# A transformer-like layer on one core: waits of the branch pool by tile, and block weights split ahead of output weights

## The chip, the cores and the metric

The kernel runs on one core of one Trainium2 chip. The metric is the device time of one execution in microseconds; the table below has it for three runs. Five engines share the work: TensorE (PE) multiplies, VectorE (DVE) and ScalarE (ACT) do elementwise work, GpSimd (POOL) a little of it, and SyncE (SP) issues nearly all DMAs. Each engine works through its own instructions in the order in which the program gives them, and waits on semaphores for the others.

## The reference

One layer with 512 tokens (T), width 1024 (D) and a hidden width of 2816 (FF), in fp32:

```
mod = silu(c) @ w_ada + b_ada                 # nine vectors: shifts, scales, gates
u = rms_norm(x) * (1 + sc1) + sh1
x = x + 0.5 * g1 * swiglu(u, ffn1_w_in, ffn1_w_out)
u = rms_norm(x) * (1 + sc2) + sh2
z = u @ w_mix + b_mix                         # q, k, v of two attentions, and gates
y_a = sigmoid(o) * rms_norm(mlstm(...))       # chunkwise mLSTM, 4 heads
y_b = forgetting_attention(...)               # 16 heads
merged = sigmoid(g_a) * (y_a @ w_branch_a) + sigmoid(g_b) * (y_b @ w_branch_b)
x = x + g2 * (merged @ w_out)
u = rms_norm(x) * (1 + sc3) + sh3
x = x + 0.5 * g3 * swiglu(u, ffn2_w_in, ffn2_w_out)
# swiglu(u, w_in, w_out) = (silu(u @ w_in_a) * (u @ w_in_b)) @ w_out
```

## The kernel before

**Products in three parts.** Each fp32 operand is split into a rounded part (hi) and a remainder (lo); a product is three matmuls, hi x hi, hi x lo and lo x hi (`mm3`, L112 to L114). For a weight, `w_stat` loads a tile `raw` of 128x1024 (three buffers, L82) and `split` (L85) makes `wh` on ScalarE (L93) and `wl` on VectorE (L95), four buffers each.

**Feed-forward stages.** FF is cut into 22 blocks of 128. `block` (L553) takes the two input weights of a block (one for each half of `w_in`), multiplies the tokens by both, 24 matmuls each, and `hidden` makes silu(a) * b of it, `hp` (L376, L377). Two blocks form a pair, whose product with the output weights saves multiplications by sums of its quarters (as in Strassen's scheme). For pair jj, `weight_load` (L404) loads the pair's output weights, 1 MB, into `rw`, which has one buffer. `weight_sums` (L414 to L422) rounds the first half of them (`wh`, `wl`) and forms four differences in place. `sums_store` (L427) writes three quarters of the tile to the DRAM buffer `S_d`, for use later. The next pair's load into `rw` can start when that store has been done. `pair_sums` (L382 to L398) makes sums and splits of `hp`. `first_products` (L434 on) multiplies them with `wh` and with the first difference. In between, `steps` puts accumulations of modulation weights (`raw` from `w_ada`, `acc`, L303 to L305) on VectorE.

`three_blocks` handles pairs 0 to 2 of the first feed-forward stage: blocks 0 to 2 are computed with the input stage, then come blocks 3, 4 and 5. `ffn_pairs` handles the others, and all of the second stage.

**Mixing and branches.** After attention, `ya` and `yb` hold the two branch inputs, eight tiles of 128x512 each. `gate(m, i)` computes a tile of the gates and stores it in DRAM (`g_d`); gate (7, 1) is the last. `split_y` (L1160, L1161) splits a branch's input. `branch(m, i)` loads a gate tile (`sg`) and multiplies the split input by a branch weight, 24 matmuls; there are eight for each branch, the first branch with y_a. These tiles live in the pool `br`, which takes the memory of the attention pools before it.

**What sets the order.** A scheduler orders the instructions of each engine from the program's order and its own rules; `issue_after(x)` puts the instructions in its scope behind x. A pool that takes over memory makes its tiles wait for the work that used it: by default for the earlier pool's work as a whole, with `reuse_waits="tile"` for that of the tiles that lay there.

Of the kernel before, what the change touches and what calls it, by code (L numbers as in the profile page):

```python
# [11 lines left out]
F32 = mybir.dt.float32  # L12
F32R = mybir.dt.float32r
# [7 lines left out]
P = 128  # L21
# [27 lines left out]
class Layer:  # L49
# [35 lines left out]
    def split(self, src, shape, eng=None, hi_v=False):  # L85
        nc = self.nc
        hi = self.wp.tile(shape, F32R, name=self.nm("wh"), tag="wh", bufs=4)
        lo = self.wp.tile(shape, F32R, name=self.nm("wl"), tag="wl", bufs=4)
        if hi_v:
            nc.vector.tensor_copy(hi, src)  # L90
        else:
            with self.tc.issue_after(self.last_uf.ins) if self.lo_after else nullcontext():
                nc.scalar.activation(hi, src, AF.Copy)  # L93
        with self.tc.issue_after(self.lo_after) if self.lo_after else nullcontext():
            self.last_lo = (eng or nc.vector).tensor_tensor(lo, src, hi, op=SUB)  # L95
        return hi, lo
# [453 lines left out]
    def block_w(self, w_in, j):  # L550
        return self.w_stat(w_in, j * P), self.w_stat(w_in, FF + j * P)

# [43 lines left out]
    def ffn_pairs(self, w_in, w_out, j0, steps, n):  # L596

        for jj in range(j0, NP):
            if jj:
                self.block(w_in, 2 * jj)  # L600
# [12 lines left out]
        self.first_products(NP - 1)  # L613
# [167 lines left out]
    def gates(self, mp, yp):  # L781
# [31 lines left out]
        def columns():  # L813
            b = self.tbank()
            for tb in range(NT):
                nc.tensor.transpose(b[:, tb * 64:(tb + 1) * 64], gm[:, tb * P:(tb + 1) * P], self.ident[:64, :64])
            self.gcol = yp.tile([P, NT, 64], F32, name="gcol")
            nc.vector.tensor_copy(self.gcol, b[:, 0:256].rearrange("p (b c) -> p b c", b=NT))
        return columns
# [44 lines left out]
    def v_mlstm(self, half, ap, ip):  # L864
# [3 lines left out]
        for i in range(2):  # L868
            pair = [ap.tile([P, NT, 258], F32R, name=self.nm("vm"), tag="vm", bufs=6) for _ in range(2)]
# [19 lines left out]
    def mlstm_w(self, h, ip):  # L889
# [7 lines left out]
        nc.gpsimd.tensor_tensor(b4(Mm), b4(Mb), self.maskM[:, None, :].to_broadcast([P, NT, P]), op=ADD)  # L897
        W = ip.tile([P, 1280], F32, name=self.nm("W"), tag="p6", bufs=5)
        Wh = ip.tile([P, 1280], F32R, name=self.nm("Wh"), tag="p6", bufs=5)
        Wl = ip.tile([P, 1280], F32R, name=self.nm("Wl"), tag="p6", bufs=5)  # L900
        for sb in range(NT):
# [46 lines left out]
    def fox_qkv(self, g, ip):  # L948
# [28 lines left out]
        bv = self.bias_bcast([(VF + o, 256)], ip)  # L977
        vt = [ip.tile([P, NT, 2, P], F32R, name=self.nm("fvt"), tag="vm", bufs=6) for _ in range(2)]
        def donev(tb, ps):
# [47 lines left out]
    def fox_s(self, h, ip):  # L1027
# [7 lines left out]
        nc.gpsimd.tensor_tensor(b4(Am), b4(A0), self.maskF[:, None, :].to_broadcast([P, NT, P]), op=ADD)  # L1035
        S = ip.tile([P, 1280], F32, name=self.nm("S"), tag="p6", bufs=5)
        mn = sp.tile([P, NT, 2], F32, name=self.nm("mn"), tag="mn", bufs=4)
# [19 lines left out]
    def fox_p(self, h, ip):  # L1057
# [7 lines left out]
        Ph = ip.tile([P, 1408], F32R, name=self.nm("Ph"), tag="p6", bufs=5)  # L1065
        Pl = ip.tile([P, 1408], F32R, name=self.nm("Pl"), tag="p6", bufs=5)
        nc.scalar.activation(Ph[:, 512:640], self.ident, AF.Copy, scale=0.0)
# [62 lines left out]
    def gate(self, m, i, ip):  # L1130
        nc = self.nc
        ps = self.gbank()
        w = self.w_stat(self.A["w_mix"][0], (GA, GB)[i] + m * P)
        self.gemm_stat(ps, w, 0, T, range(0, 4))
        yield
        self.gemm_stat(ps, w, 0, T, range(4, 8))
        th = self.tmp(ip, "tg")
        nc.scalar.activation(th, ps, AF.Tanh, scale=0.5, bias=self.hgg[:, 8 * i + m:8 * i + m + 1])
        nc.sync.dma_start(self.g_d[8 * i + m], th)
        yield  # L1140


    def branch(self, m, i, bp, dst):
# [4 lines left out]
        wh, wl = self.w_stat(A[("w_branch_a", "w_branch_b")[i]][0], m * P)  # L1148
        for k in range(NK):
            self.mm3(ps, wh[:, k, :], wl[:, k, :], self.y[k][0], self.y[k][1], k == 0, k == NK - 1)  # L1150
        dst = sg if dst is None else dst
        nc.vector.scalar_tensor_tensor(dst, sg, 1.0, ps, op0=ADD, op1=MUL)
        return dst

    def split_y(self, ys, tile):
        nc = self.nc
        out = []
        for i, y in enumerate(ys):
            hi, lo = tile(i, 0), tile(i, 1)
# [6 lines left out]
    def run(self):  # L1166
# [8 lines left out]
        with tc.tile_pool(name="f1t", bufs=1) as tp:  # L1175
# [39 lines left out]
        with tc.tile_pool(name="gates", bufs=1) as mp:  # L1215
# [5 lines left out]
            for m in range(4, 8):  # L1221
# [5 lines left out]
                self.qk_conv(m, ps, yp, mp)  # L1227
        with tc.tile_pool(name="att", bufs=1) as ip:
            self.maskM = ip.tile([P, P], F32, name="maskM")
# [8 lines left out]
            nc.gpsimd.memset(self.onz[:, :, 1:2], 0.0)  # L1238
            self.hom = ip.tile([P, NK], F32, name="hom")
            nc.vector.tensor_scalar(self.hom, self.colA[:, R_OM:R_OM + NK], 0.5, None, op0=MUL)  # L1240
            self.hgg = ip.tile([P, 2 * NK], F32, name="hgg")
            nc.vector.tensor_scalar(self.hgg, self.colA[:, R_GG:R_GG + 2 * NK], 0.5, None, op0=MUL)
# [44 lines left out]
        self.ntmp, self.xn_tiles = 4, self.xn_branch  # L1287
        with tc.tile_pool(name="br", bufs=1) as bp:
            self.tp = bp
            self.mh = [bp.tile([P, T], F32R, name=f"mh{m}") for m in range(NK)]  # L1290
            self.ml = [bp.tile([P, T], F32R, name=f"ml{m}") for m in range(NK)]
            halves = lambda: [yp.tile([P, 512], F32, name=self.nm("acc"), tag="qk", bufs=16) for _ in range(2)]
            steps = self.ada_steps((6, 7), halves, self.tbank)
            ya = self.split_y(self.ya, lambda i, lo: bp.tile([P, T], F32R, name=self.nm("yl"), tag=f"y{lo}", bufs=8))
            ta = []
# [66 lines left out]
```

## Time and profile before

| | |
|---|---|
| device time, median of 3 runs | 1353.15 us (1352.94 to 1353.87) |
| the profiled execution: device time, span | 1355.86 us, 1354.1 us |
| TensorE busy, its mean granted clock | 1321.2 us (98%), 0.989 |
| VectorE, ScalarE, GpSimd busy | 936.4 us (69%), 619.4 us (46%), 135.2 us (10%) |
| DMA, mean | 171 GB/s |

The span runs from the first to the last instruction of the profiled execution. Busy shares are means over stages that have different limits, so the rows further down are taken from single stages. The granted clock is TensorE's clock as a share of full speed. In the stretch from 73 to 320 us the kernel is in the first feed-forward stage; the branches begin at 855 us, the second feed-forward stage at about 1010 us.

### The profile page before, as it was taken

The page shows a single profiled execution, that of the slowest core. Times are in us where ns is not written, and L with a number is a line of the kernel's source. Part 1 is how long each engine was busy: PE and PEld are TensorE (multiplying, and loading weights), DVE is VectorE, ACT ScalarE, POOL GpSimd, SP SyncE. Part 2 cuts the span into 40 slices and gives each one's busy share as a digit, 9 for nine tenths or more (in the row PEclk, how much of TensorE's full clock was granted, in tenths as well). Part 3 has the DMA queues.
Part 4 walks back from the last instruction along what each step waited for, and adds up shares of the span by engine and source line. Part 5 has one row for each costly group of instructions (what it writes and reads, how often), then busy time and mean ns, then how long its engine had stood idle before and what let it go on. Part 6 is the DMA issues. An engine that isn't in the chain of part 4 may idle for free.

```text
span 1354.1 us, 17890 instructions
## 1 busy us (share of the span) xinstructions
PE 1321.2 (98%) x6438; PEld 1107.6 (82%) x6438; DVE 936.4 (69%) x1697; ACT 619.4 (46%) x1050; POOL 135.2 (10%) x175
## 2 busy tenths in 40 slices
PE   6899999999999999999999999899999999999998
PEld 5787888888888888888888878688888888888887
DVE  6685778579677876876585886567677575555655
ACT  4442343336447655556565675323444343333442
POOL 2000000001011100313031311002110000000000
PEclk9899999999999999999999999899999999999999
DMA  9566877666762434444343442587526745435474
GB/s 314 153 204 209 255 234 239 220 199 231 243 171 78 135 112 123 124 117 127 81 140 86 114 131 73 189 251 229 171 94 219 240 151 186 145 124 176 131 263 146
DMA packets 224524, 231.10 MB, mean 171 GB/s; under 512 B 12274, under 2 KB 179858, under 8 KB 224436
## 3 DMA queue, kind: packets, MB, share of 16 engines
q1 hardware_dynamic: 221940, 224.61, 52.8%
q0 software_dynamic: 2432, 5.33, 1.1%
q8 instruction: 51, 0.84, 0.2%
q14 instruction: 37, 0.30, 0.1%
q10 hardware_dynamic: 64, 0.02, 0.0%
HBM read 199.97 MB, written 29.95 MB: 170 GB/s over the span
## 4 chain that ended last, share of the span: by engine, by line
PE 82%; DVE 8%; DMA 5%; ACT 3%; issue 2%; SPq 0%; POOL 0%; ACTq 0%; DVEq 0%; POOLq 0%
PE g L113 19%; PE g L114 19%; PE g L112 19%; PE t L461 2%; PE t L463 2%; PE t L462 2%; DMA rw<-in_ffn_w_out_dram 2%; PE g L760 2%; PE t L1102 2%; DVE wl L95 1%; PE t L436 1%; PE t L434 1%; PE t L435 1%; DMA raw<-in_ffn_w_in_dram 1%; PE t L1072 1%
## 5 line engine op out<-in xcount | busy, mean ns | idle before, releaser
L93 ACT ACTIVATE wh<-raw 128x1024 fp32r<-128x1024 f32 (+2 forms) x225 | 232.0, 1037 | 347.5 <-PE g L113 102.6
L95 DVE TENSOR_TENSOR wl<-raw,wh 128x1024 fp32r<-128x1024 f32 (+2 forms) x225 | 272.7, 1216 | 155.3 <-ACT wh L93 149.6
L114 PE MATMUL g<-uh,wl 128*128 128x512 f32 (+2 forms) x984 | 369.7, 377 | 2.3 <-DVE wl L95 2.3
L112 PE MATMUL g<-uh,wh 128*128 128x512 f32 (+2 forms) x984 | 370.2, 377 | 1.2 <-ACT wh L93 1.2
L113 PE MATMUL g<-ul,wh 128*128 128x512 f32 (+2 forms) x984 | 370.0, 376 | 0.7 <-DVE ul L262 0.7
L114 PEld LDWEIGHTS g<-uh,wl 128*128 128x128 f32 (+1 forms) x984 | 184.8, 188 | 37.3 <-DVE wl L95 3.8
L112 PEld LDWEIGHTS g<-uh,wh 128*128 128x128 f32 (+1 forms) x984 | 184.7, 188 | 35.3 <-ACT wh L93 2.3
L113 PEld LDWEIGHTS g<-ul,wh 128*128 128x128 f32 (+1 forms) x984 | 185.0, 188 | 34.3 <-DVE ul L262 0.9
L112 PE MATMUL g<-wh,uh 128*128 128x512 f32 (+1 forms) x320 | 111.9, 350 | 0.0
L114 PE MATMUL g<-wh,ul 128*128 128x512 f32 (+1 forms) x320 | 111.1, 347 | 0.0
L113 PE MATMUL g<-wl,uh 128*128 128x512 f32 (+1 forms) x320 | 111.0, 347 | 0.0
L303 DVE SCALAR_TENSOR_TENSOR acc<-raw,ccol,acc 128x1024 f32<-128x1024 f32 (+1 forms) x63 | 65.9, 1062 | 28.7 <-DMA raw<-in_w_ada_dram 28.1
L377 DVE TENSOR_TENSOR hp<-g,sl 128x512 f32<-128x512 f32 x43 | 29.6, 689 | 56.6 <-PE g L114 55.5
L112 PEld LDWEIGHTS g<-wh,uh 128*128 128x128 f32 x320 | 60.5, 189 | 7.8 <-DVE tk L956 0.5
L114 PEld LDWEIGHTS g<-wh,ul 128*128 128x128 f32 x320 | 60.5, 189 | 7.7
L113 PEld LDWEIGHTS g<-wl,uh 128*128 128x128 f32 x320 | 60.6, 189 | 7.4
L112 PE MATMUL g<-yl,wh 128*128 128x512 f32 x128 | 51.2, 400 | 5.9 <-ACT yl L1160 5.9
L414 ACT ACTIVATE wh<-rw 128x1024 fp32r<-128x1024 f32 x22 | 23.3, 1059 | 63.5 <-PE g L113 36.0
L113 PE MATMUL g<-yl,wh 128*128 128x512 f32 x128 | 51.1, 399 | 0.0
L114 PE MATMUL g<-yl,wl 128*128 128x512 f32 x128 | 50.8, 397 | 0.0
L322 POOL DMA_DIRECT2D mod_d<-br x14 | 7.0, 501 | 387.3 <-DVE br L321 281.9
L1054 ACT ACTIVATE S<-S,mn 128x128 f32<-128x128 f32 (+1 forms) x64 | 35.5, 556 | 20.3 <-DVE mn L1046 12.6
(314 smaller groups left out, 2285.0 us busy)
## 6 DMA issues: line engine op xcount, KB each, us to landing
raw<-in_ffn_w_in_dram SPq DMA_DIRECT2D x82, 512.0 KB
raw<-in_w_ada_dram SPq DMA_DIRECT2D x56, 512.0 KB
raw<-in_w_mix_dram SPq DMA_DIRECT2D x48, 512.0 KB
rw<-in_ffn_w_out_dram SPq DMA_DIRECT2D x22, 1024.0 KB
S_d<-rw SPq DMA_DIRECT2D x22, 768.0 KB
raw<-S_d SPq DMA_DIRECT2D x30, 512.0 KB
raw<-in_w_mix_dram SPq DMA_DIRECT2D x32, 256.0 KB
ar<-in_w_ada_dram SPq DMA_DIRECT2D x14, 512.0 KB
```

What stands on the lines that cost most here:

```text
L93: nc.scalar.activation(hi, src, AF.Copy)
L95: self.last_lo = (eng or nc.vector).tensor_tensor(lo, src, hi, op=SUB)
L112: mm(ps, lh, rh, start=start, stop=False)
L113: mm(ps, lh, rl, start=False, stop=False)
L114: self.last_mm = mm(ps, ll, rh, start=False, stop=stop)
L303: nc.vector.scalar_tensor_tensor(a, r[:, cut(i)], self.ccol[:, k:k + 1], a, op0=MUL, op1=ADD)
L377: nc.vector.tensor_tensor(h, ps_b[:, c0:c1], s[:, :c1 - c0], op=MUL)
L461: mm(ps[t], a[0], wh[:, k, :], start=first and c + k == 0, stop=False, skip_group_check=True)
L462: mm(ps[t], a[0], wl[:, k, :], start=False, stop=False, skip_group_check=True)
L463: mm(ps[t], a[1], wh[:, k, :], start=False, stop=end, skip_group_check=True)
L760: mm = nc.tensor.matmul(acc_ps[b], (wl if p == 1 else wh)[:, b % 2, s], ul if p == 2 else uh, start=k == 0 and p == 0, stop=k == NK - 1 an ...
L1054: nc.scalar.activation(S[:, ws], S[:, ws], AF.Exp, scale=-1.0, bias=m, accum_out=sm[:, qb:qb + 1])
```

## The change

Three edits. In `three_blocks` and `ffn_pairs`, the input weights of the following block are loaded and split ahead of `weight_sums`, whose instructions are put behind the first rounding of that block's weights (`first_hi`); this holds for jj = 1 and 2 in the first stage and for jj = 0 in the second. The pool `br` waits tile by tile; gate (7, 1) is computed inside it, after the splits of y_a; the first branch weight is split ahead, and the tiles `mh`, `ml` are allocated later. The splits of y_b come in four parts of two, in the branch steps m = 1 to 4, behind the last tanh of the gates on ScalarE and behind the last y_a remainder on VectorE. Besides, some tiles move to other pools (`vp`, `yp`), and `gcol` shrinks from 64 to 36 columns.

```diff
     def block_w(self, w_in, j):
-        return self.w_stat(w_in, j * P), self.w_stat(w_in, FF + j * P)
+        wa = self.w_stat(w_in, j * P)
+        self.first_hi = self.last_hi
+        return wa, self.w_stat(w_in, FF + j * P)
...
+        w = None
         for jj in (1, 2):
-            self.block(w_in, 3 + jj)
+            self.block(w_in, 3 + jj, w)
             if jj == 2:
                 self.weight_load(w_out, 2)
                 self.first_products(1)
             steps(True, n)
-            r = self.weight_sums(jj)
+            w = self.block_w(w_in, 4 + jj)
+            with self.tc.issue_after(self.first_hi.ins):
+                r = self.weight_sums(jj)
             self.pair_sums(jj)
             self.sums_store(jj, r)
...
-            r = self.weight_sums(jj)
             if jj:
+                r = self.weight_sums(jj)
                 self.block(w_in, 2 * jj + 1)
+            else:
+                w = self.block_w(w_in, 2)
+                with self.tc.issue_after(self.first_hi.ins):
+                    r = self.weight_sums(jj)
...
-            advance(with_gates(iter(()), 1), 99)
...
-        with tc.tile_pool(name="br", bufs=1) as bp:
+        with tc.tile_pool(name="br", bufs=1, reuse_waits="tile") as bp:
...
             ya = self.split_y(self.ya, lambda i, lo: bp.tile([P, T], F32R, name=self.nm("yl"), tag=f"y{lo}", bufs=8))
+            ya_lo = self.last_lo
+            for _ in self.gate(7, 1, bp):
+                pass
+            first = self.w_stat(A["w_branch_a"][0], 0)
+            yb = []
...
-                if m == 2:
-                    yb = self.split_y(self.yb, lambda i, lo: self.up.tile([P, T], F32R, name=self.nm("yl"), tag=("uh", "ul")[lo] + str(i)))
-                ta.append(self.branch(m, 0, bp, yp.tile([P, T], F32, name=self.nm("ta"), tag="qk", bufs=16)))
+                ta.append(self.branch(m, 0, bp, yp.tile([P, T], F32, name=self.nm("ta"), tag="qk", bufs=16), first if m == 0 else None))
+                if 0 < m < 5:
+                    with tc.issue_after(self.last_th.ins), tc.issue_after(ya_lo.ins):
+                        yb += self.split_y(self.yb[2 * m - 2:2 * m], lambda i, lo: self.up.tile(
+                            [P, T], F32R, name=self.nm("yl"), tag=("uh", "ul")[lo] + str(2 * m - 2 + i)))
```

The first place is ScalarE at the start of the branches. `yl<-yb` and `yl<-ya` are roundings of the branch inputs, `tg` is the tanh of the last gate. Before:

```order
L1160 ACTIVATE yl_8281<-yb_3426 128x512
L1160 ACTIVATE yl_8285<-yb_3427 128x512
L1160 ACTIVATE yl_8289<-yb_3428 128x512
L1138 ACTIVATE tg_8130<-g_8099,hgg 128x512
L1160 ACTIVATE yl_8293<-yb_3429 128x512
L1160 ACTIVATE yl_8153<-ya_7506 128x512
L1160 ACTIVATE yl_8157<-ya_7607 128x512
L1160 ACTIVATE yl_8161<-ya_7690 128x512
```

After:

```order
L1171 ACTIVATE yl_8119<-ya_7778 128x512
L1171 ACTIVATE yl_8123<-ya_7879 128x512
L1171 ACTIVATE yl_8127<-ya_7962 128x512
L1171 ACTIVATE yl_8131<-ya_8045 128x512
L1171 ACTIVATE yl_8135<-ya_8100 128x512
L1149 ACTIVATE tg_8170<-g_8139,hgg 128x512
L1171 ACTIVATE yl_8265<-yb_3422 128x512
L1171 ACTIVATE yl_8269<-yb_3423 128x512
```

The y_a roundings moved ahead of the last gate's tanh, where the y_b roundings were, and the y_b roundings went behind it.

The second place is VectorE in the first feed-forward stage, at `weight_sums(1)`: `rw_784` is pair 1's output weights, `L95` the remainders of a block's input weights, `acc` the accumulations. Before:

```order
L415 TENSOR_TENSOR wl_884<-rw_784,wh_883 128x1024
L95 TENSOR_TENSOR wl_912<-raw_909,wh_911 128x1024
L416 TENSOR_TENSOR rw_784<-rw_784 128x512
L419 TENSOR_TENSOR rw_784<-rw_784 128x512
L95 TENSOR_TENSOR wl_918<-raw_915,wh_917 128x1024
L420 TENSOR_TENSOR rw_784<-rw_784 128x512
L421 TENSOR_TENSOR xs_889<-rw_784,xs_888 128x512
L422 TENSOR_TENSOR rw_784<-rw_784 128x512
L303 SCALAR_TENSOR_TENSOR acc_876<-raw_994,ccol,acc_876 128x1024
L303 SCALAR_TENSOR_TENSOR acc_876<-raw_997,ccol,acc_876 128x1024
L377 TENSOR_TENSOR hp_872<-g_823,sl_873 128x512
```

After:

```order
L95 TENSOR_TENSOR wl_886<-raw_883,wh_885 128x1024
L95 TENSOR_TENSOR wl_892<-raw_889,wh_891 128x1024
L415 TENSOR_TENSOR wl_896<-rw_784,wh_895 128x1024
L303 SCALAR_TENSOR_TENSOR acc_876<-raw_994,ccol,acc_876 128x1024
L416 TENSOR_TENSOR rw_784<-rw_784 128x512
L303 SCALAR_TENSOR_TENSOR acc_876<-raw_997,ccol,acc_876 128x1024
L419 TENSOR_TENSOR rw_784<-rw_784 128x512
L377 TENSOR_TENSOR hp_872<-g_823,sl_873 128x512
L420 TENSOR_TENSOR rw_784<-rw_784 128x512
L421 TENSOR_TENSOR xs_901<-rw_784,xs_900 128x512
L422 TENSOR_TENSOR rw_784<-rw_784 128x512
L95 TENSOR_TENSOR wl_1003<-raw_1000,wh_1002 128x1024
```

Both remainders of block 5 moved ahead of that of `rw`, and two accumulations and a product of `hidden` moved in between the differences (L416 to L422); a remainder of block 6 now follows them at once.

The third is SyncE's queue a little later: `S_d_679` are stores of sums, `rw_1092` is pair 2's load, `raw_1130` and `raw_1136` are block 7's weights, `raw_1209` and `raw_1212` modulation weights, `raw_1215` an input weight of block 8. Before:

```order
L404 DMA rw_974<-in_ffn_w_out_dram 128x2x1024
L82 DMA raw_1115<-in_w_ada_dram 128x1024
L427 DMA S_d_679<-rw_974 128x1536
L82 DMA raw_1130<-in_ffn_w_in_dram 128x8x128
L404 DMA rw_1092<-in_ffn_w_out_dram 128x2x1024
L82 DMA raw_1136<-in_ffn_w_in_dram 128x8x128
L82 DMA raw_1209<-in_w_ada_dram 128x1024
L82 DMA raw_1212<-in_w_ada_dram 128x1024
L82 DMA raw_1215<-in_ffn_w_in_dram 128x8x128
```

After:

```order
L82 DMA raw_1130<-in_ffn_w_in_dram 128x8x128
L404 DMA rw_974<-in_ffn_w_out_dram 128x2x1024
L82 DMA raw_1136<-in_ffn_w_in_dram 128x8x128
L82 DMA raw_1209<-in_w_ada_dram 128x1024
L82 DMA raw_1212<-in_w_ada_dram 128x1024
L427 DMA S_d_679<-rw_974 128x1536
L82 DMA raw_1215<-in_ffn_w_in_dram 128x8x128
L404 DMA rw_1092<-in_ffn_w_out_dram 128x2x1024
L82 DMA raw_1221<-in_ffn_w_in_dram 128x8x128
```

The load of `rw_1092` moved behind both modulation loads and one load of block 8.

## Rows read from the trace of the kernel before

**Rows 1.** Waits of TensorE: engine, line, waited for, us, times, longest.
```profile
PE g L112 <- ACT yl L1160: 5.9, 1, 5.9
...
PE g L114 <- DVE wl L95: 2.3, 3, 1.7
...
PE g L112 <- ACT wh L93: 1.2, 2, 1.0
...
PE t L436 <- DVE xs L391: 0.7, 1, 0.7
```

**Rows 2.** Timeline of TensorE, branch start: start, us, what, xcount, idle before.
```profile
854.61 0.39 PE L114 MATMUL g<-uh,wl 128*128 128x512 f32 x1
860.89 0.79 PE L112 MATMUL g<-yl,wh 128*128 128x512 f32 x1 [5.90 <-ACT yl L1160]
```

**Rows 3.** Windows: length, PE, PEld, DVE, ACT, POOL busy; granted clock, DMA share, GB/s.
```profile
857.00:858.00 1.00, 0.00 (x0) 0.00 (x0) 0.30 (x1) 0.00 (x0) 0.00 (x0) 0.53 0.88 207
861.00:867.00 6.00, 6.00 (x14) 4.40 (x15) 4.78 (x8) 3.48 (x7) 0.00 (x0) 0.50 0.56 183
867.00:868.00 1.00, 1.00 (x5) 0.80 (x4) 0.00 (x0) 0.00 (x0) 0.00 (x0) 0.85 0.00 0
120.56:126.00 5.44, 5.44 (x24) 4.51 (x25) 3.15 (x3) 0.12 (x1) 0.00 (x0) 1.00 0.80 278
```

**Rows 4.** Timeline of ScalarE, branch start.
```profile
850.44 4.54 ACT L1160 ACTIVATE yl<-yb 128x512 fp32r<-128x512 f32 x7
...
860.21 4.27 ACT L1160 ACTIVATE yl<-ya 128x512 fp32r<-128x512 f32 x8 [3.97 <-DMA x<-x_d]
```

**Rows 5.** Timeline of VectorE, branch start.
```profile
852.41 4.89 DVE L1161 TENSOR_TENSOR yl<-yb,yl 128x512 fp32r<-128x512 f32 x8
860.87 4.91 DVE L1161 TENSOR_TENSOR yl<-ya,yl 128x512 fp32r<-128x512 f32 x8 [3.57 <-ACT yl L1160]
```

**Rows 6.** Timeline of TensorE, first feed-forward stage.
```profile
120.56 0.51 PE L114 MATMUL g<-uh,wl 128*128 128x512 f32 x1 [1.69 <-DVE wl L95]
...
132.03 0.39 PE L112 MATMUL g<-uh,wh 128*128 128x512 f32 x1
...
159.44 0.50 PE L114 MATMUL g<-uh,wl 128*128 128x512 f32 x1 [0.48 <-DVE wl L95]
```

**Rows 7.** Chain of waits from 80 to 170 us: start, us, what.
```profile
99.72 4.16 DMA S_d<-rw
103.95 7.14 DMA rw<-in_ffn_w_out_dram
...
117.79 3.24 DMA S_d<-rw
121.10 6.91 DMA rw<-in_ffn_w_out_dram
```

**Rows 8.** Timeline of ScalarE, first feed-forward stage.
```profile
91.50 1.06 ACT L414 ACTIVATE wh<-rw 128x1024 fp32r<-128x1024 f32 x1 [1.60 <-DMA rw<-in_ffn_w_out_dram]
...
94.74 1.06 ACT L93 ACTIVATE wh<-raw 128x1024 fp32r<-128x1024 f32 x1 [0.57 <-DMA raw<-in_ffn_w_in_dram]
...
128.03 1.06 ACT L414 ACTIVATE wh<-rw 128x1024 fp32r<-128x1024 f32 x1 [1.55 <-DMA rw<-in_ffn_w_out_dram]
```

**Rows 9.** Timeline of VectorE, first feed-forward stage.
```profile
99.02 0.68 DVE L422 TENSOR_TENSOR rw<-rw 128x512 f32<-128x512 f32 x1
99.62 2.60 DVE L303 SCALAR_TENSOR_TENSOR acc<-raw,ccol,acc 128x1024 f32<-128x1024 f32 x2
...
108.66 1.28 DVE L303 SCALAR_TENSOR_TENSOR acc<-raw,ccol,acc 128x1024 f32<-128x1024 f32 x1 [5.85 <-DMA raw<-in_w_ada_dram]
...
129.12 1.22 DVE L415 TENSOR_TENSOR wl<-rw,wh 128x1024 fp32r<-128x1024 f32 x1 [5.42 <-ACT wh L414]
130.27 1.22 DVE L95 TENSOR_TENSOR wl<-raw,wh 128x1024 fp32r<-128x1024 f32 x1
```

**Rows 10.** Timeline of SyncE's queue, same stage.
```profile
102.24 0.42 SPq L82 DMA_DIRECT2D raw<-in_w_ada_dram  x1
```

More of the change, by code (lines that the diff above doesn't have):

```diff
@@ L591, in three_blocks, with ffn_pairs @@
             steps(True, n)
-            r = self.weight_sums(jj)
+            w = self.block_w(w_in, 4 + jj)
+            with self.tc.issue_after(self.first_hi.ins):
+                r = self.weight_sums(jj)
             self.pair_sums(jj)
             self.sums_store(jj, r)
-    def ffn_pairs(self, w_in, w_out, j0, steps, n):
+        return w
+    def ffn_pairs(self, w_in, w_out, j0, steps, n, w=None):
         for jj in range(j0, NP):
             if jj:
-                self.block(w_in, 2 * jj)
+                self.block(w_in, 2 * jj, w)
+                w = None
             self.weight_load(w_out, jj)
@@ L816, in columns @@
                 nc.tensor.transpose(b[:, tb * 64:(tb + 1) * 64], gm[:, tb * P:(tb + 1) * P], self.ident[:64, :64])
-            self.gcol = yp.tile([P, NT, 64], F32, name="gcol")
-            nc.vector.tensor_copy(self.gcol, b[:, 0:256].rearrange("p (b c) -> p b c", b=NT))
+            self.gcol = yp.tile([P, NT, 36], F32, name="gcol")
+            nc.vector.tensor_copy(self.gcol, b[:, 0:256].rearrange("p (b c) -> p b c", b=NT)[:, :, 0:36])
         return columns
@@ L868, in v_mlstm @@
         for i in range(2):
-            pair = [ap.tile([P, NT, 258], F32R, name=self.nm("vm"), tag="vm", bufs=6) for _ in range(2)]
+            pair = [self.vp.tile([P, NT, 258], F32R, name=self.nm("vm"), tag="vm", bufs=6) for _ in range(2)]
             nc.scalar.activation(pair[0][:, :, 256:258], self.onz, AF.Copy)
@@ L977, in fox_qkv @@
         bv = self.bias_bcast([(VF + o, 256)], ip)
-        vt = [ip.tile([P, NT, 2, P], F32R, name=self.nm("fvt"), tag="vm", bufs=6) for _ in range(2)]
+        vt = [self.vp.tile([P, NT, 2, P], F32R, name=self.nm("fvt"), tag="vm", bufs=6) for _ in range(2)]
         def donev(tb, ps):
@@ L1035, in fox_s @@
         nc.gpsimd.tensor_tensor(b4(Am), b4(A0), self.maskF[:, None, :].to_broadcast([P, NT, P]), op=ADD)
-        S = ip.tile([P, 1280], F32, name=self.nm("S"), tag="p6", bufs=5)
+        S = self.vp.tile([P, 1280], F32, name=self.nm("S"), tag="p6", bufs=5)
         mn = sp.tile([P, NT, 2], F32, name=self.nm("mn"), tag="mn", bufs=4)
@@ L1064, in fox_p @@
             nc.vector.tensor_scalar(S[:, ws], S[:, ws], sm[:, qb:qb + 1], None, op0=MUL)
-        Ph = ip.tile([P, 1408], F32R, name=self.nm("Ph"), tag="p6", bufs=5)
-        Pl = ip.tile([P, 1408], F32R, name=self.nm("Pl"), tag="p6", bufs=5)
+        Ph = self.vp.tile([P, 1408], F32R, name=self.nm("Ph"), tag="p6", bufs=5)
+        Pl = self.vp.tile([P, 1408], F32R, name=self.nm("Pl"), tag="p6", bufs=5)
         nc.scalar.activation(Ph[:, 512:640], self.ident, AF.Copy, scale=0.0)
@@ L1137, in gate, with branch @@
         th = self.tmp(ip, "tg")
-        nc.scalar.activation(th, ps, AF.Tanh, scale=0.5, bias=self.hgg[:, 8 * i + m:8 * i + m + 1])
+        self.last_th = nc.scalar.activation(th, ps, AF.Tanh, scale=0.5, bias=self.hgg[:, 8 * i + m:8 * i + m + 1])
         nc.sync.dma_start(self.g_d[8 * i + m], th)
         yield
-    def branch(self, m, i, bp, dst):
+    def branch(self, m, i, bp, dst, w=None):
         nc, A = self.nc, self.A
@@ L1227, in run @@
                 self.qk_conv(m, ps, yp, mp)
-        with tc.tile_pool(name="att", bufs=1) as ip:
+        with tc.tile_pool(name="heads", bufs=1) as self.vp, tc.tile_pool(name="att", bufs=1) as ip:
+            self.hom = yp.tile([P, NK], F32, name="hom")
             self.maskM = ip.tile([P, P], F32, name="maskM")
@@ L1238, in run @@
             nc.gpsimd.memset(self.onz[:, :, 1:2], 0.0)
[L1239 removed]
             nc.vector.tensor_scalar(self.hom, self.colA[:, R_OM:R_OM + NK], 0.5, None, op0=MUL)
[L1241 removed]
+            self.hgg = yp.tile([P, 2 * NK], F32, name="hgg")
             nc.vector.tensor_scalar(self.hgg, self.colA[:, R_GG:R_GG + 2 * NK], 0.5, None, op0=MUL)
@@ L1294, in run @@
             ya = self.split_y(self.ya, lambda i, lo: bp.tile([P, T], F32R, name=self.nm("yl"), tag=f"y{lo}", bufs=8))
+            ya_lo = self.last_lo
[3 more added lines that the diff above has]
+            yb = []
+            self.mh = [bp.tile([P, T], F32R, name=f"mh{m}") for m in range(NK)]
+            self.ml = [bp.tile([P, T], F32R, name=f"ml{m}") for m in range(NK)]
             ta = []
```

20 lines of the change are left out of this document (9 added, 11 removed).

## The prediction

> **What bounds the kernel now.** I read the waits of TensorE first. TensorE is the busy engine of this kernel, so a change can only win or lose time where TensorE stands still or runs at its lower clock. The reader is to see four groups [rows 1]: one wait of 5.9 us for `yl`, three for `wl` of together 2.3 us, two for `wh` of 1.2 us, one for `xs` of 0.7 us. The edits touch the places of exactly these; nearly all of the rest is the start of the kernel, which they leave as it is. Next come the timelines around the waits, and the windows with the granted clock beside them, since a wait can cost more than its length. Last I read the chain of waits from 80 to 160 us, which shows what the waits of the first feed-forward stage hang on: the load of the output weights `rw`, which has one buffer.
>
> **The branch start (parts 2 and 3 of the change), a gain.** TensorE's last gate matmul starts at 854.61, the first of the branch at 860.89, after 5.90 us of waiting for `yl` [rows 2]. ScalarE shows why: it rounded seven tiles of y_b from 850.44 on, while the y_a tiles, which the first branch multiplies, started only at 860.21, 3.97 us idle before them, released by the loads `x<-x_d` [rows 4]. VectorE did the same: eight y_b remainders at 852.41, y_a at 860.87 [rows 5]. So y_a had two things ahead of it: y_b in the order, and a wait for everything that lived in the old pool, late DMAs included.
> The wait also cost clock. The granted clock is 0.53 between 857 and 858, 0.50 from 861 to 867, 0.85 from 867 to 868 [rows 3]; 0.5 of full speed is 1.2 of 2.4 GHz. A stretch at clock c loses 1 - c of its length: 0.11 x 0.5 + 6 x 0.5 + 1 x 0.15 = 3.2 us. The count agrees: 14 matmuls in those 6 us are 0.43 us each, and 24 in 5.44 us at full clock are 0.227 [rows 3]. Price of the place: 5.9 + 3.2 = 9.1 us.
> The order after the change puts eight y_a roundings right behind the last tanh of the stage before, and no DMA ahead of them. Eight took 4.27 us, about 0.57 apart, and their remainders 4.91, or 0.61 apart [rows 4, 5]. From 850.44 on the k-th remainder is done by 852.4 + 0.61 (k + 1). TensorE, going on at 855.0, needs the k-th tile at 855.0 + 0.68 k, three matmuls of 0.227 each. It is never late, by at least 2 us. The y_b splits, now in pieces behind, have until the second branch. What is late next is the fourth branch weight: I lay ScalarE's queue out by these durations and find it ready 1 to 2 us before it is needed, so I cost that at nothing; without this cover it would cost that one rounding, about 1 us. Bounds: 9.1 gained if all goes, 5.9 if something holds TensorE long enough to keep the lower clock, 0 if a new wait takes the place. I take -9.1.
>
> **The first feed-forward stage (part 1), a loss.** Before, the rounding of output weights stood ahead of the next block's input weights; now behind the first of them. What this removes: 0.7 us (`xs`), 1.69 at 120.56 and 0.48 at 159.44 [rows 1, 6], because block 6 has its weights early. Together 2.9 us.
> What it adds lies in the chain of `rw`. One buffer means: load, round, four differences, store to `S_d`, and only then the next load. Rows 7 show it: store at 99.72 (4.16), load at 103.95 (7.14), store at 117.79 (3.24), load at 121.10 (6.91). Before, nothing stood between. Now:
> Block 5's two roundings come ahead of that of `rw`, which goes from 91.50 to the end of the second, 94.74 + 1.06 = 95.8 [rows 8]. On VectorE two remainders are ahead, then the remainder of `rw`, and two accumulations of 1.25 us each (2.60 for two) and one product come between the differences, of 0.60 each [rows 9]. From 97.0, the end of block 5's second remainder: 1.15 + 1.25 + 0.6 + 1.25 + 0.6 + 0.6 + 3 x 0.6 gives 104.3 for the last difference, against 99.7. So 4.6 us later.
> The store then takes 3.24 to 4.16 [rows 7], so the next load starts at 107.6 to 108.5, and at the 7 us of its two rows lands at 115. Its rounding, remainder and sums, with `pl` and one accumulation now among them, take 1.07 + 1.15 + 0.9 (`pl`, three quarters as wide as a remainder) + 0.6 + 1.25 + 2.4 = 7.4; the store starts at 122.5 and is done at 126.0.
> The third load starts there, against 121.10, and lands at 132.9. Block 7's roundings still stand behind the rounding of this `rw`. Before, the rounding was at 128.03 and block 7's first remainder, 1.22 at 130.27, ended 3.5 us after it [rows 8, 9]. Now it ends at 136.4.
> TensorE reaches block 7 at 132.03 less the two waits removed ahead of it, 2.43: 129.6 [rows 6]. Four matmuls of 0.227 need only the rounded halves, 0.9 us. The stall is 136.4 - 129.6 - 0.9 = 5.9 us, nearly all in one piece.
> That is as long as the wait of rows 2, behind which the clock fell; after the 1.69 us at 120.56 it stayed at 1.00 [rows 3]. By the nearer row the clock falls here too, for 3.0 us, a bit under the 3.2 above, since part of its slow time is spent waiting. Sum: 5.9 - 2.9 + 3.0 = +6.0 us.
> The size of the load decides. Above it is bounded by 7.14; below by the store, three quarters of the bytes in 3.24 us, so 4.3 for all of them. At 4.3 the stall is 3.3 us and the clock may hold: then +0.4. I take the rows of the load itself.
> The Trainium skill, page "DMA: Bandwidth & Descriptors", section "Anatomy of one DMA", fits a transfer as about 2 us fixed plus the bytes at 436 GB/s. For this 1 MB load that would be an estimated 4.4 us, near the lower bound, and the sum of the stage +0.5; the load's own rows at 7.14 and 6.91, with other loads in flight, differ, and I go by them. The same page, "Rules for kernel authors", advises to issue a DMA early and wait for it late; this edit goes against it for `rw`, whose loads start later.
>
> **The second feed-forward stage**, one place of the same edit. TensorE waits there twice for `wh`, 1.2 us [rows 1], on the second `rw`. The last difference now has one accumulation more ahead of it (1.28 us [rows 9]) and one short sum fewer: about 1 us later, and with no slack TensorE waits 1.0 us more. Bounds: 1.2 gained, and 1.0 + 3.2 lost if the clock falls. I take +1.0.
>
> **Attention.** Pools and fills of masks move, and the gate's column tile shrinks; no group of rows 1 lies there that the edit touches. Cover is TensorE's gapless stretch; without it, under 1 us either way. Zero.
>
> **Sum.** -9.1 + 6.0 + 1.0 = -2.1 us. The profiled execution took 1355.86 us, its span 1354.1; it lies 0.2% above the median of 1353.15, with the same stages, so the difference is taken off the median: 1351.0 us. About 0.2%, 2.7 us, is what a measurement tells from no change.
>
> **Rivals.**
> (a) The third load is quick, 4.3 us, the clock holds: -9.1 + 0.4 + 1.0 = -7.7, so 1345.4. For it: fewer loads share the queue at 126 than at 121. Against: two rows at about 7.
> (b) The feed-forward stalls vanish altogether, since my laid-out queue is too pessimistic by 6 us: -9.1 - 2.9 + 1.0 = -11.0, so 1342.2. Against: the one buffer and three queues in series, which I see no way around.
> (c) Slower: SyncE now has block 8's input load ahead of the third `rw` load, and that waits for an accumulation on a modulation weight. Such a load, issued at 102.24, released VectorE at 108.66 [rows 9, 10], 6.4 us. At this price the accumulation ends at 127.9, the load starts at 128.0, lands at 135.1, and the stall is 8.1 us: 8.1 - 2.9 + 3.2 = +8.4. That alone makes -9.1 + 8.4 + 1.0 = +0.3; if the later loads lag by the same 2 us in the second stage with the lower clock, 3.2 more: +3.5, so 1356.7. It decides from a third load that lands after 135. For it: no slack in the chain. Against: little else is in flight at 120.
> (d) The branch gap stays, by a wait for one late tile: 0 + 6.0 + 1.0, so 1360.2. Against: no DMA stands before the y_a splits in the order.
>
> **How the numbers follow.** Forecast 0.40 (own range 1348.5 to 1353.5, somewhat under half of it faster by 0.2%), (a) 0.27, (b) 0.12, (c) 0.13 (half of it slower), (d) 0.08. Faster: 0.17 + 0.27 + 0.12 = 0.56. Same: 0.23 + 0.06 = 0.29. Slower: 0.07 + 0.08 = 0.15. The range leaves out (b) and (d): from just under (a) to (c), 1345 to 1356.7.
>
> **What would show it.** Branch: TensorE's wait for `yl` gone, granted clock 1.00 from 855 on. First stage: the waits for `xs` and the one at 120.56 gone, a new one of 4 to 7 us at about 130 before block 7, released by `wh` or `wl`, with the clock at 0.5 behind it; stores to `S_d` at about 104 and 122, the third `rw` load at about 126. Second stage: the wait near 1040 about 2 us. The forecast is wrong if the third load starts before 123, if block 7 doesn't wait, or if a wait at the branch remains.

## The result and the profile after

The changed kernel takes 1356.08 us in the median of 17 runs (1353.69 to 1359.85), the kernel before 1353.03 us in 17 runs beside it (1351.51 to 1355.21). The ratio is 1.0025, its 95% interval 1.0017 to 1.0033: slower by about 3 us, where 2 us faster was forecast. The profiled execution has a span of 1356.1 us at a mean granted clock of 0.989.

TensorE's waits in the changed kernel (columns as in [rows 1]):

```profile
PE g L112 <- ACT wh L93: 10.9, 2, 6.9
...
PE g L114 <- DVE wl L95: 0.2, 1, 0.2
```

The wait for `yl` is gone, and those for `xs` and `wl` nearly so. One line has taken their place: two waits for `wh`, 10.9 us together. The timeline of TensorE shows where they are, which is where [rows 6] have block 7 starting without a wait, and where the second stage waited 1.2 us, in two pieces, before:

```profile
134.10 0.79 PE L112 MATMUL g<-uh,wh 128*128 128x512 f32 x1 [6.89 <-ACT wh L93]
...
1040.58 0.80 PE L112 MATMUL g<-uh,wh 128*128 128x512 f32 x1 [3.96 <-ACT wh L93]
```

Windows of the changed kernel (columns as in [rows 3]):

```profile
131.00:132.00 1.00, 0.00 (x0) 0.00 (x0) 0.00 (x0) 0.00 (x0) 0.00 (x0) 0.80 0.05 20
132.00:134.00 2.00, 0.00 (x0) 0.00 (x0) 0.87 (x1) 1.96 (x3) 0.00 (x0) 0.50 0.00 0
134.00:140.00 6.00, 5.90 (x17) 4.47 (x18) 6.00 (x8) 2.57 (x4) 0.00 (x0) 0.63 0.50 139
140.00:141.00 1.00, 1.00 (x6) 0.83 (x5) 0.77 (x2) 0.00 (x0) 0.00 (x0) 1.00 0.51 205
850.00:870.00 20.00, 20.00 (x90) 16.29 (x89) 15.65 (x25) 10.65 (x19) 1.01 (x1) 1.00 0.62 196
1039.00:1040.00 1.00, 0.00 (x0) 0.00 (x0) 0.39 (x1) 1.00 (x2) 0.00 (x0) 0.77 0.03 8
1041.00:1045.00 4.00, 4.00 (x10) 2.89 (x10) 4.00 (x6) 2.05 (x3) 0.00 (x0) 0.50 0.46 129
1046.00:1047.00 1.00, 1.00 (x5) 0.82 (x4) 1.00 (x2) 0.00 (x0) 0.00 (x0) 0.81 0.77 299
```

From 850 to 870, the branch start, the clock is 1.00 and TensorE is busy throughout; compare [rows 3]. Instead, it is at 0.50 in and behind both new waits. In the first place TensorE is busy for nearly all of the 6 us from 134, so that place lost (1 - 0.63) x 6 = 2.2 us. In the second the clock was at 0.50 from the first matmul at 1040.58 until 1046 and at 0.81 in the window behind: 5.4 x 0.5 + 0.2 = 2.9 us.

The branch start on ScalarE and VectorE, which answers to [rows 4, 5]:

```profile
854.15 4.26 ACT L1171 ACTIVATE yl<-ya 128x512 fp32r<-128x512 f32 x8
858.78 0.69 ACT L1149 ACTIVATE tg<-g,hgg 128x512 f32<-128x512 f32 x1 [0.36 <-PE g L114]
859.36 4.27 ACT L1171 ACTIVATE yl<-yb 128x512 fp32r<-128x512 f32 x8
...
856.12 4.90 DVE L1172 TENSOR_TENSOR yl<-ya,yl 128x512 fp32r<-128x512 f32 x8
```

The eight y_a roundings start at 854.15, right behind the ScalarE instruction before them and with no wait ahead. The tanh of the last gate (`tg`) and the y_b roundings come behind them.

The chain of waits of the changed kernel, from 80 to 170 us, answers to [rows 7]:

```profile
102.49 3.67 DMA S_d<-rw
106.18 7.11 DMA rw<-in_ffn_w_out_dram
...
120.94 3.28 DMA S_d<-rw
124.28 7.74 DMA rw<-in_ffn_w_out_dram
```

Each piece starts later than before: the store at 102.49 against 99.72, the load of pair 3's weights at 124.28 against 121.10. (Ahead of the prediction a sentence calls `rw_1092` pair 2's load; it is pair 3's.) The last piece is also longer, 7.74 us against 6.91.

To see how much each stage changed, I compare the start times of the same ScalarE instruction in both traces, after minus before. Each line has this difference at its end and, in bold, what it grew by over the line:

| from where to where (times of before) | difference at the end, us: growth | forecast |
|---|---|---|
| until 70 us, before the change can act | -1.8 (one execution against another) | 0 |
| first feed-forward stage, to 318 us | +3.5: **+5.3** | +6.0 |
| attention, to 855 us | +3.75: **+0.3** | 0 |
| branches and the first 9 us of the output product (from 952), to 961 us | -3.7: **-7.5** | -9.1 |
| the rest of the output product, to 1001 us | -3.2: **+0.5** | 0 |
| second feed-forward stage, from 1048 us on | +2.0: **+5.2** | +1.0 |

Without the first line the sum is +3.8, beside +3.05 between the medians. These are single executions. In the kernels further down that keep a stage's order the first stage comes out at -1.6 to +0.5 us against the kernel before, and the second at 0.0 to +0.6, so neither growth is chance. The start times of TensorE's matmuls, compared by their number from the start, give the same for both stages, and the figures by stage of the experiments below are taken from them.

### The profile page after: what moved, and what is told of

Same layout as the page of the kernel before. It is cut to its first block, busy times and chain, and to the rows that moved or that the text cites. A ratio compares the mean times of both kernels' runs of the same rounds, so it can differ in the third digit from the quotient of the medians.

```text
span 1356.1 us, 17885 instructions
## 1 busy us (share of the span) xinstructions
PE 1321.5 (97%) x6438; PEld 1107.1 (82%) x6438; DVE 937.4 (69%) x1697; ACT 618.7 (46%) x1050; POOL 136.5 (10%) x175
## 4 chain that ended last, share of the span: by engine, by line
PE 85%; DVE 6%; DMA 5%; ACT 2%; issue 2%; SPq 0%; POOL 0%; ACTq 0%; DVEq 0%; POOLq 0%
PE g L113 20%; PE g L112 20%; PE g L114 20%; PE t L461 2%; PE t L462 2%; PE t L463 2%; DMA rw<-in_ffn_w_out_dram 2%; PE g L771 2%; PE t L1113 2%; PE t L435 1%; PE t L434 1%; PE t L436 1%; PE t L112 1%; PE t L113 1%; PE t L114 1%
## 5 line engine op out<-in xcount | busy, mean ns | idle before, releaser
L95 DVE TENSOR_TENSOR wl<-raw,wh 128x1024 fp32r<-128x1024 f32 (+2 forms) x225 | 273.6, 1219 | 162.0 <-ACT wh L93 152.2
L112 PE MATMUL g<-uh,wh 128*128 128x512 f32 (+2 forms) x984 | 372.5, 379 | 10.9 <-ACT wh L93 10.9
```

Source lines behind the costliest of these rows:

```text
L95: self.last_lo = self.last_wl = (eng or nc.vector).tensor_tensor(lo, src, hi, op=SUB)
L112: mm(ps, lh, rh, start=start, stop=False)
```

## The experiments

All but the last two were run 5 to 12 times beside the kernel before on the same chip; ratios are to that kernel, whose median was 1353.5 to 1353.9 in these runs. A kernel's profile is that of one of its executions.

**The parts apart.** Two kernels: one with the changed branch alone (the lines below and their like in `ffn_pairs` undone), one with the changed feed-forward order alone.

```diff
-            w = self.block_w(w_in, 4 + jj)
-            with self.tc.issue_after(self.first_hi.ins):
-                r = self.weight_sums(jj)
+            r = self.weight_sums(jj)
```

> Parts 2 and 3 alone (branch pool, last gate, splits of y_b); both feed-forward stages as before. Theory, from the traces of before and after: the loss sits wholly in the feed-forward reorder, so this run has the branch gain alone: the wait of 5.9 us for yl and its lower clock gone, about 2 us given back in slower branch and output matmuls, so 7 us less than before, 1346. Rival: the move of the pools disturbs the feed-forward stages too, and the time is near that of the changed kernel, 1356.

> Part 1 alone (next block's weights ahead of weight_sums), the branch as before. Theory: the new stalls before block 7 (about 7 us) and in the second stage (about 4 us), with the clock at 0.5 behind both, less the 2.9 us of stalls removed, stand in full: 10 us slower than before, 1363. Rival: the stalls depend on where the run stands when it gets there, and the edit alone costs less than 3 us, 1356 or below.

The branch alone: 1347.55 us, ratio 0.9952 (0.9938 to 0.9967), 6.5 us faster. The feed-forward order alone: 1362.48 us, ratio 1.0054 (1.0040 to 1.0068), 7 us slower by the ratio and 8.6 by the medians. TensorE in the kernel with the feed-forward order alone:

```profile
135.75 0.80 PE L112 MATMUL g<-uh,wh 128*128 128x512 f32 x1 [8.54 <-ACT wh L93]
...
868.39 0.79 PE L112 MATMUL g<-yl,wh 128*128 128x512 f32 x1 [6.22 <-ACT yl L1171]
...
1049.64 0.68 PE L112 MATMUL g<-uh,wh 128*128 128x512 f32 x1 [3.42 <-ACT wh L93]
```

It has both new waits and still the old one at the branch. The theory holds, though the feed-forward order costs 7 to 9 us and not 10: the loss is the feed-forward order's, the gain the branch's. By the medians they add up to -6.4 + 8.6 = +2.2, beside +3.05 for both together.

**Why the load of output weights is late in the second stage.** In the changed kernel SyncE issues an input-weight load right ahead of it, and it takes long (SyncE's queue and ScalarE):

```profile
1030.04 0.38 SPq L82 DMA_DIRECT2D raw<-in_ffn_w_in_dram  x1
1030.83 0.38 SPq L404 DMA_DIRECT2D rw<-in_ffn_w_out_dram  x1
...
1038.52 1.06 ACT L414 ACTIVATE wh<-rw 128x1024 fp32r<-128x1024 f32 x1 [8.82 <-DMA rw<-in_ffn_w_out_dram]
```

From issue to rounding: 7.7 us. The same load in the kernel before, with a modulation-weight load ahead of it, took 5.6:

```profile
1032.66 0.34 SPq L82 DMA_DIRECT2D raw<-in_w_ada_dram  x1
1033.10 0.39 SPq L404 DMA_DIRECT2D rw<-in_ffn_w_out_dram  x1
...
1038.71 1.06 ACT L414 ACTIVATE wh<-rw 128x1024 fp32r<-128x1024 f32 x1 [6.39 <-DMA rw<-in_ffn_w_out_dram]
```

The forecast gave this load no change. The other traces agree: in the five with the new order of this place (the changed kernel and the runs with the feed-forward order alone, with the two other addresses and with the sums first) it took 6.5 to 8.1 us, in the six with the old order 5.6 to 5.9. The experiment puts the input-weight loads of the block that comes next behind it, in the first stage (block 8) and in the second (block 4):

```diff
-                self.nc.sync.dma_start(dst(t), src)
+            with self.tc.issue_after(self.rw_dma.ins) if self.after_rw else nullcontext():
+                self.nc.sync.dma_start(dst(t), src)
...
+                self.after_rw = jj == (4 if j0 else 2)
                 self.block(w_in, 2 * jj, w)
+                self.after_rw = False
```

> The changed kernel with two input-weight loads (block 8 of the first stage, block 4 of the second) issued behind the output-weight load that they stood right ahead of. Theory: the output-weight load takes 7.6 us because it comes right behind a load of input weights, and 5.5 without it; the stall before block 7 falls from 6.9 to about 4.8, that of the second stage from 4.0 to about 2, there without the lower clock: 7 us less than the changed kernel, 1349. Rival: the load takes 7 to 8 us wherever it stands, as the other rows of about 7 say; no change, 1356.

1351.38 us, ratio 0.9978 (0.9966 to 0.9990): 4.7 us less than the changed kernel by the medians, 6.4 by the ratios, where 7 were expected. The same place in this kernel:

```profile
1029.45 0.38 SPq L406 DMA_DIRECT2D rw<-in_ffn_w_out_dram  x1
1029.93 0.42 SPq L84 DMA_DIRECT2D raw<-in_ffn_w_in_dram  x1
...
1034.40 1.06 ACT L416 ACTIVATE wh<-rw 128x1024 fp32r<-128x1024 f32 x1 [6.07 <-DMA rw<-in_ffn_w_out_dram]
...
1036.46 0.50 PE L114 MATMUL g<-uh,wh 128*128 128x512 f32 x1 [1.33 <-ACT wh L95]
...
1037.40 0.50 PE L114 MATMUL g<-uh,wh 128*128 128x512 f32 x1 [0.21 <-ACT wh L95]
```

```profile
1037.00:1044.00 7.00, 6.79 (x23) 5.22 (x23) 6.13 (x8) 1.93 (x3) 0.00 (x0) 0.76 0.55 156
```

The load takes 4.95 us and the wait is 1.33 + 0.21 us and not 3.96. One part of the expectation missed: the clock falls behind this short wait too, to 0.76 over the next 7 us, which loses (1 - 0.76) x 7 = 1.7 us. The second stage loses 1.9 us against the kernel before, where the changed kernel lost 5.2. So the order of loads is the cause of the long wait there, and what is left is nearly all clock.

In the first stage the load takes 5.15 us (124.44 to 129.59), and the wait before block 7 is 5.23 us, still with the clock at 0.50 behind it: there the load starts late as well. This stage loses 4.6 us where the changed kernel lost 5.3, so the order of loads is the smaller part of its loss; an input-weight load stood right ahead of this load before the change too, when it took 6.9 us. What makes the first stage's load vary stays open: with the same queue order it took 7.8 us in the changed kernel and 6.0 in the run with aligned tiles below, and 7.9 with a modulation-weight load 1.1 us ahead in the run with one place alone.

**What delays the chain.** The prediction blamed the accumulations that come among the differences of the output weights. Here they come behind:

```diff
-            steps(True, n)
             w = self.block_w(w_in, 4 + jj)
             with self.tc.issue_after(self.first_hi.ins):
                 r = self.weight_sums(jj)
+            steps(True, n)
```

> The changed kernel with the accumulations of modulation weights put behind the output weights' differences in the first stage (pairs 1 and 2) instead of among them. Theory: the two accumulations of 1.25 us at each pair are a third to a half of what the chain loses; without them the store of pair 1 starts 2.5 us sooner, the load of pair 3 about 4 us sooner, at 120 instead of 124, and the stall before block 7 falls from 6.9 to about 3 us, with no or half the loss of clock: 4 to 6 us less than the changed kernel, 1351. Rival: the order of roundings on ScalarE alone sets the delay: a stall of 6 to 7 us, 1356.

1354.0 us (1348.85 to 1358.65 in 12 runs), ratio 0.9997 (0.9982 to 1.0013): 2 us less than the changed kernel by the medians, 4 by the ratios, with a wide spread. In the profiled execution the store of pair 1 starts at 99.61, the load of pair 3 at 121.34, and the wait falls as expected:

```profile
128.95 0.50 PE L112 MATMUL g<-uh,wh 128*128 128x512 f32 x1 [2.24 <-ACT wh L93]
...
129.90 0.80 PE L112 MATMUL g<-uh,wh 128*128 128x512 f32 x1 [0.22 <-ACT wh L93]
```

```profile
129.00:131.00 2.00, 1.78 (x5) 1.15 (x6) 2.00 (x4) 1.79 (x2) 0.00 (x0) 0.65 0.00 0
131.00:136.00 5.00, 5.00 (x19) 4.01 (x18) 4.63 (x6) 0.63 (x1) 0.00 (x0) 0.80 0.71 209
```

But the clock falls behind this wait of 2.24 + 0.22 us too, to 0.65 and 0.80: the price of a short wait was too low. The step on VectorE's queue stands, since the store and the load moved as it says. The time shows less than the trace: the profiled execution, at 1350.4 us, is as fast as expected, but the median is 3.6 us above it, and what the slower executions lost no trace shows.

**One place alone.** The branch parts, with block 6's weights ahead of `weight_sums(2)` as the one reorder that is left (its lines against those of the kernel before):

```diff
-            r = self.weight_sums(jj)
+            if jj == 2:
+                w = self.block_w(w_in, 6)
+                with self.tc.issue_after(self.first_hi.ins):
+                    r = self.weight_sums(jj)
+            else:
+                r = self.weight_sums(jj)
```

> The branch parts with the reorder at one place alone: block 6's weights ahead of weight_sums of pair 2; pair 1 and the second stage as before. Theory: what costs is the delay that pair 1 puts into the chain of output-weight loads; without it the load of pair 3 starts near 121, as before, and the stalls of together 2.4 us ahead of block 7 shrink to 0 to 2 us without loss of clock: 1 us less than the branch parts alone, 1346.5. Rival: each reorder costs by itself, since the loads of pair 3 still come later: a stall of 4 us or more before block 7, 1350 or more.

1349.9 us, ratio 0.9978 (0.9969 to 0.9988), 2.4 to 3.5 us more than the branch alone. The time is that of the rival, the wait lies between the two theories:

```profile
130.99 0.50 PE L112 MATMUL g<-uh,wh 128*128 128x512 f32 x1 [2.66 <-ACT wh L93]
...
131.94 0.49 PE L112 MATMUL g<-uh,wh 128*128 128x512 f32 x1 [0.22 <-ACT wh L93]
```

```profile
131.00:133.00 2.00, 1.78 (x5) 0.99 (x6) 2.00 (x4) 1.84 (x2) 0.00 (x0) 0.95 0.00 0
133.00:137.00 4.00, 4.00 (x12) 3.10 (x12) 4.00 (x6) 0.63 (x1) 0.00 (x0) 0.60 0.78 229
```

The waits removed ahead of block 7 come back as one of 2.66 + 0.22 us, and the clock falls behind it: (1 - 0.60) x 4 = 1.6 us. In the profiled execution of the branch-only kernel the waits of this stage are 1.10 us at 116.54 and 0.57 us at 155.51. So even this place costs more than it removes, and it does so without the delay of pair 1.

**The branch's missing 1.6 us.** The forecast price of the branch was 9.1, and 7.5 came. The matmuls of the first branch became slower without any wait: 0.234 us from one to the next where it was 0.227. In the built programs (their addresses are not in the traces) the split tiles of the branch pool lie at other addresses, which leave 96 when divided by 256 and not 192: `hom`, 32 bytes, went into the pool below. Two kernels move them, the first to multiples of 64 bytes (they leave 128), the second back to addresses that leave 192:

```diff
-            self.hom = yp.tile([P, NK], F32, name="hom")
+            self.hom = yp.tile([P, 16], F32, name="hom")
...
-            self.hom = yp.tile([P, NK], F32, name="hom")
+            self.hom = yp.tile([P, 32], F32, name="hom")
```

> The changed kernel with the tile hom made 16 columns wide instead of 8, so that the tiles of the branch pool lie at multiples of 64 bytes again instead of 32 beyond one; nothing else moves. Theory: a matmul that reads an operand 32 bytes off takes 0.234 instead of 0.227 us; 192 of the first branch and 192 of the output product go back to 0.227, 2.5 us in all: 1353.5, 0.2% below the changed kernel. Rival: those matmuls are slowed by the denser transfers and splits around them; spacing stays 0.234, time 1356.

> The changed kernel with hom 32 columns wide, which puts the split tiles of the branch pool at addresses that leave 192 when divided by 256, as all fast operands of the traces do (the input of the gates, the weights, and these tiles before the change). Theory: the place within 256 bytes decides, not within 64: the matmuls of the first branch and of the output product take 0.227 us again instead of 0.234, 2.5 us in all, 1353.5. Rival: the place doesn't matter, and what lies beside these matmuls does: 0.234 as in the two runs before, 1355 to 1356.

1354.96 us, ratio 1.0007 (0.9996 to 1.0017), and 1355.3 us, ratio 1.0014 (1.0004 to 1.0025): both medians about 1 us under the changed kernel, with intervals that touch its own, and the medians do not tell them from each other or from the rivals. The matmuls do. The window from 865 to 895, all in the first branch, of the changed kernel, the first and the second:

```profile
865.00:895.00 30.00, 30.00 (x130) 24.12 (x129) 20.67 (x29) 5.30 (x5) 0.00 (x0) 1.00 0.91 280
```

```profile
865.00:895.00 30.00, 30.00 (x131) 24.02 (x130) 18.73 (x26) 6.42 (x7) 0.00 (x0) 1.00 0.90 277
```

```profile
865.00:895.00 30.00, 30.00 (x134) 24.86 (x133) 20.62 (x29) 5.81 (x6) 0.00 (x0) 1.00 0.87 275
```

TensorE is busy throughout in each; there are 130, 131 and 134 matmuls in the same 30 us, and in the timelines of the branch their starts are 0.234, 0.233 and 0.227 us apart. From the start of the branches to the end of the output product the trace of the second gains 9.4 us against the kernel before, that of the changed kernel 6.9: the 2.5 us that were expected, which the medians do not show. The theory of 64 bytes falls for these matmuls, and that of the place within 256 fits them. The built program of the kernel before agrees: its split branch tiles, the output product's and the weights all leave 192. A second place agrees as well: in the first feed-forward stage the split hidden tiles `ph` and `pl` leave 224, in the second 192, and the matmuls of the output weights that read them start 0.233 and 0.227 us apart in the trace of before.

**A kernel faster than both.** The branch parts alone, with both groups of tiles at 192 (`warm` lies below `ph` and `pl`):

```diff
-            self.hom = yp.tile([P, NK], F32, name="hom")
+            self.hom = yp.tile([P, 32], F32, name="hom")
...
-        warm = tp.tile([P, 1], F32, name="warm")
+        warm = tp.tile([P, 64], F32, name="warm")
```

> The branch parts alone, with the tiles of the branch pool and the split hidden tiles of the first feed-forward stage both at 192 within 256 bytes. Theory (place within 256 bytes): 384 matmuls of branch and output product and about 200 of the first stage's output product go from 0.234 to 0.227 us, 4 us in all: 1343.5. Rival: 1347.5, as the branch parts alone.

1343.17 us in 5 runs (1340.5 to 1346.3), ratio 0.9934 (0.9920 to 0.9949): 9 us faster than before by the ratio, and 13 us below the changed kernel by the medians. Against the branch parts alone it is 4.4 us less by the medians and 2.4 by the ratios, where 4 were expected. In its trace the matmuls that read `ph` and `pl` start 0.227 us apart, but a wait of 1.0 us for a split weight, new there, takes that group's gain back.

**The two halves of the branch change.** One execution each of the kernel before with tile-wise waits alone, and with the new place of the y_b splits alone.

```diff
-        with tc.tile_pool(name="br", bufs=1) as bp:
+        with tc.tile_pool(name="br", bufs=1, reuse_waits="tile") as bp:
...
-                if m == 2:
-                    yb = self.split_y(self.yb, lambda i, lo: self.up.tile([P, T], F32R, name=self.nm("yl"), tag=("uh", "ul")[lo] + str(i)))
+                if 0 < m < 5:
+                    with tc.issue_after(self.last_th.ins), tc.issue_after(ya_lo.ins):
+                        yb += self.split_y(self.yb[2 * m - 2:2 * m], lambda i, lo: self.up.tile(
+                            [P, T], F32R, name=self.nm("yl"), tag=("uh", "ul")[lo] + str(2 * m - 2 + i)))
```

> The kernel before with one word changed: the branch pool waits tile by tile; its tiles, the last gate and the splits of y_b stay where they were. Theory: the wait before the branch has two causes in a row, eight y_b splits ahead in the order and the pool's wait for late transfers; with the second eased alone, the y_a roundings start when the y_b roundings end, near 856.2 instead of 860.2, and TensorE waits about 2 us instead of 5.9, without the lower clock: 1347 in one look. Rival: the first y_a tile still lies on a tile that a late transfer holds, so the wait stays at 4 to 6 us with the lower clock, 1353.

> The kernel before with the splits of y_b alone changed, to four parts behind the last tanh and the last y_a remainder; pool and last gate as before. Theory: the pool-wide wait sets the start of the y_a roundings by itself, so the wait for yl stays at 4 to 6 us, with the lower clock, 1353 in one look. Rival: order was the cause, and the wait falls below 2 us, 1346.

1354.62 and 1353.14 us, beside 1356.89 of the kernel before; single executions of that kernel differ by more than this, so the traces have to tell. TensorE and ScalarE with tile-wise waits alone:

```profile
859.11 0.79 PE L112 MATMUL g<-yl,wh 128*128 128x512 f32 x1 [6.01 <-ACT yl L1160]
...
853.72 0.62 ACT L1160 ACTIVATE yl<-yb 128x512 fp32r<-128x512 f32 x1
858.43 4.27 ACT L1160 ACTIVATE yl<-ya 128x512 fp32r<-128x512 f32 x8 [4.09 <-DMA g_d<-tg]
```

and with the new y_b splits alone:

```profile
857.69 0.79 PE L112 MATMUL g<-yl,wh 128*128 128x512 f32 x1 [4.41 <-ACT yl L1160]
...
853.32 0.69 ACT L1138 ACTIVATE tg<-g,hgg 128x512 f32<-128x512 f32 x1 [4.49 <-PE g L114]
853.90 3.21 ACT L1160 ACTIVATE yl<-yb 128x512 fp32r<-128x512 f32 x6
857.02 4.26 ACT L1160 ACTIVATE yl<-ya 128x512 fp32r<-128x512 f32 x8
```

With tile-wise waits alone the first y_a rounding waits 4.09 us, by the profile for the store of the last gate's tile. The rival was right. With the y_b splits alone, six of them still come ahead of y_a in the order, behind the last tanh, and the wait stays at 4.41 us. That is the length that its theory gave, but not by its cause: ScalarE has no idle time before y_a here, so the order set the start. Of the 7.9 us that the changed kernel gains from 853 us to the end of the second branch, the first gains 0.2 and the second 1.5. Neither is enough alone. The change does both and also moves the tiles and the last gate; how much of it is needed beyond these two was not tried.

## Why the prediction was wrong

**Right.** The places. The branch wait and its lower clock went, and with the tiles back at 192 the branches gain 9.3 us, where 9.1 was the price. In the first stage the chain went as laid out: stores forecast at 104.3 and 122.5, and the load at 126.0, were at 104.3, 122.7 and 126.1 if the 1.8 us by which this execution was earlier are added. A wait of 6.9 us came before block 7 (5.9 forecast), the clock fell behind it, and the stage lost 5.3 us (6.0 forecast). That the sum came so near is in part luck: the wait was 1.0 us longer, the lower clock cost 2.2 and not 3.0, and the waits that went gave TensorE 3.6 us by its start times, not the 2.9 that the rows of waits add up to. The rule of the Trainium skill's page "DMA: Bandwidth & Descriptors", section "Rules for kernel authors", to issue a DMA early, pointed the right way here: the load that starts later ends in a wait. The prediction also takes an estimate of 4.4 us for the 1 MB load from the section "Anatomy of one DMA" of the same page of the Trainium skill. That section is about DMAs that GpSimd issues, and SyncE issues these. The estimate lies below every load of output weights measured here for which ScalarE waited: 4.9 to 8.4 us from issue to rounding.

**The step that failed** is the second feed-forward stage, "I take +1.0". It measured +5.2. The prediction had the delay of the sums (1 us; 1.2 in the traces). It gave the load itself no change, though the new order of SyncE's queue sets an input-weight load 0.8 us ahead of it: 5.6 us became 7.7, and 4.95 with the other order of loads. The wait so came to 3.96 us, 2.8 more than before, and the clock fell behind it, 2.9 us more; together that is 5.7, half a microsecond above what the start times show. The upper bound that was written down and not taken, 1.0 + 3.2, has the clock's fall but not the longer load, and 5.2 lies above even that. Rival (c) came nearest in the time, 1356.7, but in the first stage not by its mechanism: the load before block 7 did not start late behind an accumulation, it took longer. What it adds for the second stage, a load about 2 us later with the lower clock, is what happened there.

**The second miss** is a term that was not in the sum. The prediction opens by saying that time is won or lost only where TensorE stands still or runs at its lower clock. In the branches it did neither and lost time: 7.5 came and not 9.1, since moved pools put operands at addresses where matmuls take 3% longer at a clock of 1.00. That is 192 x 0.007 = 1.3 us in the first branch, and the output product, whose operand moved too, lost about 0.3 us up to the table's 961 us and 0.5 from there on. The prediction asked of the moved pools only what waits they bring.

Together: 4.2 us in the second stage, 1.6 in the branches, 0.5 in the output product and 0.3 in attention, less 0.7 in the first stage, is 5.9 us, from -2.1 to +3.8.

## What to carry over

When an edit moves work ahead of the consumer of a single-buffered tile, follow the whole cycle of that buffer, and in the new order of the DMA queue look at what now stands right ahead of its load. Price a new wait of TensorE together with its clock: behind 4 us of waiting 2.9 us more were lost here, and behind 1.5 us of it 1.7. After a pool moves, compare the addresses of matmul operands, since their cost shows in no wait.

## What was not expected of the hardware

Matmuls of 512 columns that read an operand at an address that leaves 192 within 256 bytes started 0.227 us apart, those at 96 or 128 or 224 (for the branch's moving operand and the hidden tiles) 0.233 to 0.234; for the output product's stationary operand 0.227 at 192, 0.229 at 128 and 0.233 at 96. Which property of the address counts, other than these values, was not tried: the place within 128 bytes (64, against 0 and 96) would fit them as well.

And the granted clock fell to 0.5 behind waits of 2.24 + 0.22 and 2.66 + 0.22 us and, with the other order of loads, behind 1.33 + 0.21 us at 1036.46. It stayed at 1.00 behind the 1.69 us at 120.56 [rows 3, 6], and with the branch parts alone behind 1.58 + 0.22 us at 1031.56. So a wait's price here has a step of 1.6 to 3 us in it that its length does not tell.
